# Input squares on two engines, first weights held back, rows in turn for the gates, last projection in three token parts

## The chip, the cores and the metric

The kernel runs on one core of a Trainium2 chip. The metric is the device time of one execution in microseconds (us), and a kernel's time is the median of its runs. The profile is of one execution, taken by the hardware profiler; its span starts with the first instruction and ends with the last.

Names used below: PE is TensorE (the matrix engine), PEld its weight loads, DVE is VectorE, ACT is ScalarE, POOL is GpSimd, SP is SyncE, which here only issues DMAs. SBUF is the core's memory, PSUM the eight banks into which PE writes. A DMA is issued on the queue of an engine, and an instruction that issues a DMA may first wait for a buffer to come free; everything behind it on that engine then waits too.

## The reference

The reference is a decoder trunk of two layers on 512 tokens of width 1024, all in float32. The first layer mixes tokens with a gated DeltaNet (8 query and key heads, 16 value heads of 128, chunks of 64 in the reference), the second with sliding-window attention on shared keys and values. Each layer ends with a gated channel mixer of width 2816.

```python
h = x
h = h + gated_deltanet(rmsnorm(h, a_norm_w), ...)       # layer 0
h = h + conv_gated_mlp(rmsnorm(h, ffn_norm_w[0]), ...)
k_sh, v_sh = shared_kv(h, kv_norm_w, w_kv)
h = h + sliding_window_sink_attention(rmsnorm(h, b_norm_w), k_sh, v_sh, ...)   # layer 1
h = h + conv_gated_mlp(rmsnorm(h, ffn_norm_w[1]), ...)
return rmsnorm(h, final_norm_w)

# inside gated_deltanet, after the recurrence has given o for each of the 16 value heads:
o = rmsnorm(o, out_norm_w) * silu(z)
return o.reshape(bsz, t, GDN_V_DIM) @ w_out
```

## The kernel before

Activations stand transposed, with 128 channels on the partitions and the 512 tokens along the row. A float32 product is made of three products: weights and activations are each split into a high part, rounded by ACT (`whi`, `xh`), and the rest, subtracted by DVE (`wlo`, `xl`), and PE runs high by high, high by low and low by high into one PSUM bank (`mm3`, L158 to L165). Weights come as blocks of 1024 rows by 256 columns into one of two stages (`load_stage`) and are split in halves of 128 columns (`cast`, L128 to L134) into three buffers each for `whi` and `wlo`.

An engine's order of issue comes from a scheduler that lists the instructions by priority (by default their order in the program, shifted by hand for the jobs of the first layer in `ORDER` and `SHIFT`) and takes those that its model of time holds ready. Tiles with one tag share a fixed number of buffers; a new tile of a tag takes a buffer once all uses of an older one are over.

**Input.** Four tiles of 128 tokens are loaded on SP (L204), then the first projection's weights in two halves (L210). Each tile is squared and summed along its row by ACT (L258), ACT takes the root (L259), DVE the reciprocal (L260) and the scaling (L261). PE transposes the tiles into eight rows (L266), ACT and DVE split them (L172, L173), and the projections follow.

**Gates.** The DeltaNet's outputs go to memory as `od` by chunk, the gate projections silu(z) as `zd` by head. `gate(h)` (L711 to L727) loads a head's outputs into an output row (L716) and its gate into a second row (L717), ACT scales the outputs (L720), PE transposes them (L198, `turn_row`), DVE multiplies by the gate (L723), and the result goes to memory as `yd` (L725). For the first twelve heads the output row has the tag `ol` and the gate row the tag `zl`, each with one buffer; the last four use other rows. Before the output projection of this layer, the twelve results are read back (L824) into rows `sz` (two buffers, shared with the gate projections) and `zl`, and split (L168, L169). The residual stream starts as x, loaded by columns into eight rows (L843): three of tag `f`, which has three buffers, three pieces of a third stage, and again two of tag `f`. The first six are held until the norms of heads 8 to 11 are there, by copies on POOL that read `f_c` (L839); PE transposes them (L198) and ACT copies the result (L846).

**Attention output.** The last tokens' values are split (L168, L169) while the first three tiles of the output projection are already open in the three PSUM banks of tag `d`. Their last key block of nine products (L1380) runs in three rounds over the three tiles, high by high, low by high, high by low; after a tile's last product DVE adds it to the residual (L1382). The next five tiles go through `mm3`.

**Tail.** In the last channel mixer, the last tile of the down projection (`last_down`, L962 to L964, ten blocks of three products, in two groups of six and four) is run on tokens 0 to 255 and then on 256 to 511. After each half `finish(u)` squares the new row (L1131), multiplies it by the norm's weight (L1132), adds the square to the sum over the other rows (L1133), transposes four rows for each of two token blocks (L1118, bank `d` or `s`), sums over the partitions with a column of ones (L1137), takes the root (L1138) and the reciprocal (L1139), scales the two halves of the channels on ACT (L1144) and DVE (L1146), and stores them (L1147).

Of the kernel before, what the change touches and what calls it, by code (L numbers as in the profile page):

```python
# [11 lines left out]
AF = mybir.ActivationFunctionType  # L12
ALU = mybir.AluOpType
# [4 lines left out]
P = 128  # L18
# [23 lines left out]
def kernel(  # L42
# [64 lines left out]
    def row(tag, dt=F32, n=T):  # L107
        return main.tile([P, n], dt, tag=tag, bufs=ROWS[tag], name=nm(tag))
# [4 lines left out]
    def bank(tag):  # L113
        return psum.tile([P, T], F32, tag=tag, bufs=BANKS[tag], name=nm(tag))

    def const(shape, dt=F32, s="c"):
        return cp.tile(list(shape), dt, name=nm(s))
# [87 lines left out]
        xs.append(xt)  # L205
    win = a_w_in[0]
    first = wpool.tile([P, 8, 256], F32, tag="stage", bufs=2, name=nm("stage"))
    for i in range(2):
        cs = slice(HQK * P + i * P, HQK * P + (i + 1) * P)
        SP.dma_start(first[:, :, i * P : (i + 1) * P], win[:, cs].rearrange("(k p) c -> p k c", p=P))  # L210
# [44 lines left out]
    for c in range(NC):  # L255
        junk = main.tile([P, D], F32, tag="nt", bufs=2, name=nm("junk"))
        r = const([P, 1], s="rx")
        S.activation(junk[:], xs[c], AF.Square, accum_out=r[:])  # L258
        S.activation(r[:], r[:], AF.Sqrt, bias=epsc[:, 0:1], scale=1.0 / D)  # L259
        V.reciprocal(r[:], r[:])  # L260
        V.tensor_scalar(xs[c][:], xs[c][:], r[:, 0:1], None, op0=ALU.mult)  # L261
# [447 lines left out]
    gated = {}  # L709

    def gate(h):  # L711
        ot = row("ol" if h < 12 else "dt")
        y = row("zl") if h < 12 else row(("va", "va", "us", "p6s")[h - 12])
        o3 = ot[:].rearrange("p (c e) -> p c e", c=NC)
        j = h % 4
        SP.dma_start(o3, od[h // 4, :, :, j * P : (j + 1) * P])  # L716
        SP.dma_start(y[:], zd[h])  # L717
        for c in range(NC):
            cs = slice(c * P, (c + 1) * P)
            scaled = S.activation(ot[:, cs], ot[:, cs], AF.Copy, scale=f_c[:, h, c : c + 1])  # L720
# [379 lines left out]
    def final(h, last_down):  # L1100
        hw, acc = [], None
        for k in range(KD):
            t = r2("xh")
            hw.append(t)
            if k == KD - 1:
                break
            V.tensor_scalar(t[:], h[k], onw_c[:, 9 + k : 10 + k], None, op0=ALU.mult)
            sq = r2("sum" if acc is None else "hsq")
            S.activation(sq[:], h[k], AF.Square)
            if acc is None:  # L1110
                acc = sq
            else:
                V.tensor_tensor(acc[:], acc[:], sq[:], op=ALU.add)

        def turned(hf, c, tag):
            pt = bank(tag)
            for k in range(4):
                PE.transpose(pt[:, k * P : (k + 1) * P], hw[4 * hf + k][:, c * P : (c + 1) * P], ident[:])  # L1118
            return pt

        halves = [bank("d") for _ in range(2)]
        S.activation(warm[:], acc[:, 0:1], AF.Sqrt)
        front = [turned(0, c, t) for c, t in enumerate(["s", "s", "p", "g"])]
        h7, w7 = h[KD - 1], hw[KD - 1]
        sq7 = r2("hsq")
        rt = const([P, NC], s="rt")
        ts = [slice(0, 256), slice(256, 512)]

        def finish(u):
            cs = slice(2 * u, 2 * u + 2)  # L1130
            S.activation(sq7[:, ts[u]], h7[:, ts[u]], AF.Square)  # L1131
            V.tensor_scalar(w7[:, ts[u]], h7[:, ts[u]], onw_c[:, 16:17], None, op0=ALU.mult)  # L1132
            V.tensor_tensor(acc[:, ts[u]], acc[:, ts[u]], sq7[:, ts[u]], op=ALU.add)  # L1133
            back = [turned(1, 2 * u, "d"), turned(1, 2 * u + 1, "s" if u else "d")]
            ps = bank("g")
            for c in (2 * u, 2 * u + 1):
                PE.matmul(ps[:, c : c + 1], acc[:, c * P : (c + 1) * P], onec, start=True, stop=True)  # L1137
            S.activation(rt[:, cs], ps[:, cs], AF.Sqrt, bias=epsc[:, 0:1], scale=1.0 / D)  # L1138
            V.reciprocal(rt[:, cs], rt[:, cs])  # L1139
            for c in (2 * u, 2 * u + 1):  # L1140
                for hf, pt in enumerate((front[c], back[c % 2])):
                    y = r2("xl")
                    if hf:
                        S.activation(y[:], pt[:], AF.Copy, scale=rt[:, c : c + 1])  # L1144
                    else:
                        V.tensor_scalar(y[:], pt[:], rt[:, c : c + 1], None, op0=ALU.mult)  # L1146
                    SP.dma_start(out[0, c * P : (c + 1) * P, hf * T : (hf + 1) * T], y[:])  # L1147

        def add(u):
            V.tensor_tensor(h7[:, ts[u]], h7[:, ts[u]], halves[u][:, 0:256], op=ALU.add)  # L1150
# [12 lines left out]

    def attention(h):
# [192 lines left out]
        with tc.manual_schedule(engines={mybir.EngineType.PE}):  # L1357
            stream = dense()
            for u in range(16):
                scores(u)  # L1360
                if u > 1:
                    values(u - 2)
                if u == 1:
                    take(stream, 8)
                if u > 0:
                    turn_back(u - 1)
                take(stream, 4 if u == 1 else 12 if u < 12 else 11)
            for _ in stream:
                pass
            rest = late_outputs(opened, range(begun, KD - 1))  # L1370
            take(rest, 9)
            turn_back(15)
            values(14)
            take(rest, 5)
            values(15)
            for _ in rest:
                pass
            for i in range(3):
                for m, (ps, w) in enumerate(opened):
                    PE.matmul(ps[:], w[i % 2][:, KD - 1, :], (ah, ah, al)[i][-1], start=False, stop=i == 2)  # L1380
                    if i == 2:
                        V.tensor_tensor(hT[m], hT[m], ps[:], op=ALU.add)  # L1382
        for m in range(3, KD):
            ps, w = out_tile(m)
            mm3(ps[:], w, KD, ah, al)
# [59 lines left out]
```

## Time and profile before

| | us |
|---|---|
| median of 3 runs (1415.42 to 1416.30) | 1415.86 |
| the profiled execution | 1418.66 |
| its span | 1416.8 |
| PE busy | 1384.8 |
| DVE busy | 1109.1 |
| ACT busy | 748.0 |
| POOL busy | 15.7 |

The page of the profile gives the busy time of each engine, the chain of work that ended last, the costliest groups of instructions, and the DMAs. A row of the order of time reads: start, duration, engine, line, operation, output<-input, shape, count, and in brackets how long the engine stood idle before it and what ended that. A row of the list of waits reads: engine, tile and line that waited, what it waited for, total us, times, longest. In a row of the windows come the stretch, then for each engine busy time and count, PE's granted clock, the DMAs' share and GB/s. PE's products overlap, so the pace of a row of products is read from start to start and not from the duration of one. A product of two float32 operands that are not split has two records.

### The profile page before, as it was taken

How to read it: one execution, taken by the hardware profiler on the slowest of the kernel's cores; microseconds unless marked ns; L12 is line 12 of the kernel's file. 1: busy time of each engine (PE TensorE's matmuls, PEld its weight loads, DVE VectorE, ACT ScalarE, POOL GpSimd, SP SyncE). 2: the span in 40 equal slices, each digit the busy share in tenths (PEclk: the TensorE clock that was granted, in tenths of full speed). 3: DMA queues.
4: the chain of work that ended last, by engine and by line, in shares of the span. 5: the costliest groups of instructions: out<-in, count | busy, mean ns of one | idle time of the engine just before them, and what ended most of it. 6: DMA issues, size and time to landing. Idle time of an engine off the chain costs nothing.

```text
span 1416.8 us, 21740 instructions
## 1 busy us (share of the span) xinstructions
PE 1384.8 (98%) x8362; PEld 1166.5 (82%) x8362; DVE 1109.1 (78%) x2072; ACT 748.0 (53%) x1470; POOL 15.7 (1%) x37
## 2 busy tenths in 40 slices
PE   7999999999999999999999999999999999999997
PEld 5787888878877888888988889778788888988897
DVE  4996886968856447879878889788658888878996
ACT  7764576656647325444335446567544444444543
POOL 1000000000100000000000000000000000000000
PEclk9999999999999999999999999999999999999999
DMA  5333254172465323221443223322132221432222
GB/s 160 90 104 115 80 174 124 60 230 84 143 221 157 119 86 115 90 90 46 134 149 119 75 73 108 109 76 76 60 112 86 93 90 59 137 107 86 95 75 75
DMA packets 162299, 151.80 MB, mean 107 GB/s; under 512 B 24148, under 2 KB 150677, under 8 KB 162197
## 3 DMA queue, kind: packets, MB, share of 16 engines
q1 hardware_dynamic: 159938, 150.22, 33.0%
q8 instruction: 66, 1.08, 0.3%
q10 hardware_dynamic: 2259, 0.20, 0.1%
q14 instruction: 36, 0.29, 0.1%
HBM read 133.60 MB, written 15.75 MB: 105 GB/s over the span
## 4 chain that ended last, share of the span: by engine, by line
PE 85%; DVE 7%; DMA 4%; ACT 2%; issue 1%; SPq 0%; DVEq 0%; ACTq 0%
PE d L162 20%; PE d L164 20%; PE d L163 20%; PE g L198 2%; DVE wlo L133 2%; PE d L1207 1%; PE d L1211 1%; PE d L1209 1%; PE d L1054 1%; PE d L1052 1%; PE d L1053 1%; PE s L1054 1%; PE p L1303 1%; PE s L659 1%; PE s L1052 1%
## 5 line engine op out<-in xcount | busy, mean ns | idle before, releaser
L162 PE MATMUL d<-xh,whi 128*128 128x512 f32 x1128 | 444.2, 394 | 0.2
L163 PE MATMUL d<-xl,whi 128*128 128x512 f32 x1128 | 444.0, 394 | 0.0
L164 PE MATMUL d<-xh,wlo 128*128 128x512 f32 x1128 | 442.1, 393 | 0.8 <-DVE wlo L133 0.5
L132 ACT CAST whi<-stage 128x1024 fp32r<-128x1024 f32 (+2 forms) x234 | 227.4, 976 | 249.7 <-PE d L163 170.3
L133 DVE TENSOR_TENSOR wlo<-stage,whi 128x1024 fp32r<-128x1024 f32 (+2 forms) x234 | 263.3, 1128 | 70.2 <-ACT whi L132 69.3
L164 PEld LDWEIGHTS d<-xh,wlo 128*128 128x128 f32 x1128 | 211.6, 188 | 45.5 <-DVE wlo L133 1.0
L162 PEld LDWEIGHTS d<-xh,whi 128*128 128x128 f32 x1128 | 211.7, 188 | 44.8 <-ACT xh L172 0.5
L163 PEld LDWEIGHTS d<-xl,whi 128*128 128x128 f32 x1128 | 211.7, 188 | 43.1 <-issue 0.5
L280 DVE SCALAR_TENSOR_TENSOR acc<-d,cwc,acc 128x511 f32<-128x511 f32 (+2 forms) x96 | 70.6, 738 | 8.7 <-ACT acc L277 7.8
L913 DVE TENSOR_TENSOR sz<-d,p6s 128x512 f32<-128x512 f32 x59 | 40.6, 688 | 43.4 <-PE d L164 41.2
L935 ACT ACTIVATE dt<-dt 128x512 f32<-128x512 f32 x44 | 27.8, 632 | 78.3 <-DVE dt L918 78.3
L918 DVE SCALAR_TENSOR_TENSOR dt<-sz,fcw,dt 128x511 f32<-128x511 f32 (+1 forms) x60 | 44.8, 747 | 1.8 <-ACT dt L916 0.9
L918 DVE SCALAR_TENSOR_TENSOR va<-sz,fcw,va 128x511 f32<-128x511 f32 (+1 forms) x58 | 43.3, 747 | 0.9
L561 DVE TENSOR_TENSOR sT<-sT,p6s 64x31 f32<-64x31 f32 (+15 forms) x124 | 40.9, 330 | 2.0
L555 DVE TENSOR_TENSOR p6s<-sN,sT 64x31 f32<-64x31 f32 (+15 forms) x124 | 40.7, 328 | 1.9
L1276 ACT ACTIVATE dt<-dt,sm 128x256 f32<-128x256 f32 (+1 forms) x64 | 30.1, 471 | 21.5 <-DVE sm L1259 21.5
L132 ACT CAST whi<-st 128x768 fp32r<-128x768 f32 (+1 forms) x30 | 23.7, 791 | 30.1 <-PE p L1053 5.8
L913 DVE TENSOR_TENSOR zl<-d,p6s 128x512 f32<-128x512 f32 x29 | 20.0, 688 | 17.8 <-PE d L164 17.8
L682 ACT ACTIVATE rq<-o 128x128 f32<-128x128 f32 x64 | 19.0, 301 | 25.0 <-DVE o L677 22.0
L937 DVE TENSOR_TENSOR va<-dt,va 128x512 f32<-128x512 f32 x44 | 30.4, 690 | 1.2
L133 DVE TENSOR_TENSOR wlo<-st,whi 128x768 fp32r<-128x768 f32 (+1 forms) x30 | 26.8, 899 | 2.2 <-ACT whi L132 2.2
L916 ACT ACTIVATE dt<-sz,normc,fcw 128x512 f32<-128x512 f32 x30 | 24.4, 815 | 6.5 <-DVE sz L913 6.2
(769 smaller groups left out, 2873.2 us busy)
## 6 DMA issues: line engine op xcount, KB each, us to landing
stage<-in_ffn_w_up_dram SPq DMA_DIRECT2D x44, 1024.0 KB, 4.7
stage<-in_a_w_in_dram SPq DMA_DIRECT2D x23, 1024.0 KB, 5.5
stage<-in_ffn_w_down_dram SPq DMA_DIRECT2D x16, 768.0 KB, 4.3
stage<-in_a_w_out_dram SPq DMA_DIRECT2D x8, 1024.0 KB, 5.1
st<-in_ffn_w_down_dram SPq DMA_DIRECT2D x8, 768.0 KB, 5.2
zd<-sz SPq DMA_DIRECT2D x16, 256.0 KB, 2.6
od<-o SPq DMA_DIRECT2D x16, 256.0 KB
stage<-in_b_w_q_dram SPq DMA_DIRECT2D x4, 1024.0 KB, 5.0
```

Source lines behind the costliest of these rows:

```text
L132: S.copy(hi[:, :kt, :m], src)
L133: V.tensor_tensor(lo[:, :kt, :m], src, hi[:, :kt, :m].bitcast(F32), op=ALU.subtract)
L162: PE.matmul(ps, hi[:, k, :m], xh[k], start=first and k == 0, stop=False)
L163: PE.matmul(ps, hi[:, k, :m], xl[k][:], start=False, stop=False)
L164: done.append(PE.matmul(ps, lo[:, k, :m], xh[k], start=False, stop=last and k == kt - 1))
L280: V.scalar_tensor_tensor(acc[:, d:], ps[:, : T - d], col, acc[:, d:], op0=ALU.mult, op1=ALU.add)
L555: V.tensor_tensor(tv, N[:, s, s + 1 : 32].unsqueeze(2).to_broadcast([64, n, m]), Tm[:, s : s + 1, 0:m].to_broadcast([64, n, m]), op=ALU.mult,)
L561: V.tensor_tensor(Tm[:, s + 1 : 32, 0:m], Tm[:, s + 1 : 32, 0:m], tv, op=ALU.subtract)
L913: V.tensor_tensor(u[:], ps[:], rs[:], op=ALU.mult)
L918: V.scalar_tensor_tensor(acc[:, d:], u[:, : T - d], tap(2 - d, t), acc[:, d:], op0=ALU.mult, op1=ALU.add)
L937: V.tensor_tensor(b[:], a[:], b[:], op=ALU.mult)
L1276: S.activation(ej, ej, AF.Exp, bias=ngm[:, i : i + 1], scale=-1.0, accum_out=den[:, i : i + 1])
```

## The change

Five edits:

1. The first weights are no longer issued right behind x. POOL first copies a column of the third x tile into one element of each half of the weights' stage; the loads of the halves must then wait for these copies. The identity is made before that.
2. The squares of x tiles 1 and 3 are taken by DVE with one multiply-and-sum; those of tiles 0 and 2 stay on ACT.
3. `gate(h)` takes its output row from the tags `ol` and `zl` in turn for the first twelve heads, and its gate row from tag `f`, which has three buffers.
4. The last tile of the down projection runs in three token parts of 256, 128 and 128. A part's `finish` runs behind the first group of products of the next part. The square of the new row is not added to the sum; PE sums both rows into the same bank.
5. The last key block of the three open tiles in the attention output runs tile by tile, each tile's addition right behind its three products.

```diff
     first = wpool.tile([P, 8, 256], F32, tag="stage", bufs=2, name=nm("stage"))
+    held_stage = {HQK * P: first}
+    ident = const([P, P], s="ident")
+    make_identity(nc, ident[:])
+    for i in range(2):
+        G.tensor_copy(first[:, 0, i * P : i * P + 1], xs[2][:, 0:1])
     for i in range(2):
         cs = slice(HQK * P + i * P, HQK * P + (i + 1) * P)
         SP.dma_start(first[:, :, i * P : (i + 1) * P], win[:, cs].rearrange("(k p) c -> p k c", p=P))
-    held_stage = {HQK * P: first}
-    ident = const([P, P], s="ident")
-    make_identity(nc, ident[:])
...
-        S.activation(junk[:], xs[c], AF.Square, accum_out=r[:])
+        if c % 2 == 0:
+            S.activation(junk[:], xs[c], AF.Square, accum_out=r[:])
+        else:
+            V.tensor_tensor_reduce(
+                out=junk[:], in0=xs[c][:], in1=xs[c][:], scale=1.0, scalar=0.0,
+                op0=ALU.mult, op1=ALU.add, accum_out=r[:],
+            )
...
-        ot = row("ol" if h < 12 else "dt")
-        y = row("zl") if h < 12 else row(("va", "va", "us", "p6s")[h - 12])
+        ot = row(("ol", "zl")[h % 2] if h < 12 else "dt")
+        y = row("f" if h < 12 else ("va", "va", "us", "p6s")[h - 12])
...
-        halves = [bank("d") for _ in range(2)]
+        CUTS = [(0, 2), (2, 3), (3, 4)]
+        parts = [bank("d") for _ in CUTS]
...
-        ts = [slice(0, 256), slice(256, 512)]
+        ts = [slice(a * P, b * P) for a, b in CUTS]
         def finish(u):
-            cs = slice(2 * u, 2 * u + 2)
+            c0, c1 = CUTS[u]
+            cs = slice(c0, c1)
+            V.tensor_scalar(w7[:, ts[u]], h7[:, ts[u]], onw_c[:, 16:17], None, op0=ALU.mult)
             S.activation(sq7[:, ts[u]], h7[:, ts[u]], AF.Square)
-            V.tensor_scalar(w7[:, ts[u]], h7[:, ts[u]], onw_c[:, 16:17], None, op0=ALU.mult)
-            V.tensor_tensor(acc[:, ts[u]], acc[:, ts[u]], sq7[:, ts[u]], op=ALU.add)
-            back = [turned(1, 2 * u, "d"), turned(1, 2 * u + 1, "s" if u else "d")]
+            back = [turned(1, c, "d") for c in range(c0, c1)]
             ps = bank("g")
-            for c in (2 * u, 2 * u + 1):
-                PE.matmul(ps[:, c : c + 1], acc[:, c * P : (c + 1) * P], onec, start=True, stop=True)
+            for c in range(c0, c1):
+                for x in (acc, sq7):
+                    PE.matmul(ps[:, c : c + 1], x[:, c * P : (c + 1) * P], onec, start=x is acc, stop=x is sq7)
...
-        last_down(halves[0][:, 0:256], ts[0], 0)
-        last_down(halves[0][:, 0:256], ts[0], 1)
-        add(0)
-        last_down(halves[1][:, 0:256], ts[1], 0)
-        finish(0)
-        last_down(halves[1][:, 0:256], ts[1], 1)
-        add(1)
-        finish(1)
+        n = len(CUTS)
+        for u in range(n):
+            ps = parts[u][:, 0 : ts[u].stop - ts[u].start]
+            last_down(ps, ts[u], 0)
+            if u > 0:
+                finish(u - 1)
+            last_down(ps, ts[u], 1)
+            V.tensor_tensor(h7[:, ts[u]], h7[:, ts[u]], ps, op=ALU.add)
+        finish(n - 1)
...
-            for i in range(3):
-                for m, (ps, w) in enumerate(opened):
+            for m, (ps, w) in enumerate(opened):
+                for i in range(3):
                     PE.matmul(ps[:], w[i % 2][:, KD - 1, :], (ah, ah, al)[i][-1], start=False, stop=i == 2)
-                    if i == 2:
-                        V.tensor_tensor(hT[m], hT[m], ps[:], op=ALU.add)
+                V.tensor_tensor(hT[m], hT[m], ps[:], op=ALU.add)
```

More of the change, by code (lines that the diff above doesn't have):

```diff
@@ L257 @@
         r = const([P, 1], s="rx")
-        S.activation(junk[:], xs[c], AF.Square, accum_out=r[:])
+        if c % 2 == 0:
+            S.activation(junk[:], xs[c], AF.Square, accum_out=r[:])
+        else:
+            V.tensor_tensor_reduce(
+                out=junk[:],
+                in0=xs[c][:],
+                in1=xs[c][:],
+                scale=1.0,
+                scalar=0.0,
+                op0=ALU.mult,
+                op1=ALU.add,
+                accum_out=r[:],
+            )
         S.activation(r[:], r[:], AF.Sqrt, bias=epsc[:, 0:1], scale=1.0 / D)
@@ L1126, in final @@
         rt = const([P, NC], s="rt")
-        ts = [slice(0, 256), slice(256, 512)]
+        ts = [slice(a * P, b * P) for a, b in CUTS]
         def finish(u):
-            cs = slice(2 * u, 2 * u + 2)
+            c0, c1 = CUTS[u]
+            cs = slice(c0, c1)
+            V.tensor_scalar(w7[:, ts[u]], h7[:, ts[u]], onw_c[:, 16:17], None, op0=ALU.mult)
             S.activation(sq7[:, ts[u]], h7[:, ts[u]], AF.Square)
-            V.tensor_scalar(w7[:, ts[u]], h7[:, ts[u]], onw_c[:, 16:17], None, op0=ALU.mult)
-            V.tensor_tensor(acc[:, ts[u]], acc[:, ts[u]], sq7[:, ts[u]], op=ALU.add)
-            back = [turned(1, 2 * u, "d"), turned(1, 2 * u + 1, "s" if u else "d")]
+            back = [turned(1, c, "d") for c in range(c0, c1)]
             ps = bank("g")
-            for c in (2 * u, 2 * u + 1):
-                PE.matmul(ps[:, c : c + 1], acc[:, c * P : (c + 1) * P], onec, start=True, stop=True)
+            for c in range(c0, c1):
+                for x in (acc, sq7):
+                    PE.matmul(ps[:, c : c + 1], x[:, c * P : (c + 1) * P], onec, start=x is acc, stop=x is sq7)
             S.activation(rt[:, cs], ps[:, cs], AF.Sqrt, bias=epsc[:, 0:1], scale=1.0 / D)
             V.reciprocal(rt[:, cs], rt[:, cs])
-            for c in (2 * u, 2 * u + 1):
-                for hf, pt in enumerate((front[c], back[c % 2])):
+            for c in range(c0, c1):
+                for hf, pt in enumerate((front[c], back[c - c0])):
                     y = r2("xl")
```

2 lines of the change are left out of this document (removed).

## The prediction

> **What bounds the kernel now.** I read the page's engine shares first, then its chain of waits, then the list of what TensorE (PE) waited for, and only then the order of time at the four places that the diff touches.
>
> ```profile
> PE 1384.8 (98%) x8362; PEld 1166.5 (82%) x8362; DVE 1109.1 (78%) x2072; ACT 748.0 (53%) x1470; POOL 15.7 (1%) x37
> PE 85%; DVE 7%; DMA 4%; ACT 2%; issue 1%; SPq 0%; DVEq 0%; ACTq 0%
> ...
> PE g L235 <- DMA xt<-in_x_dram: 8.5, 1, 8.5
> ...
> PE d L162 <- ACT kT L168: 2.0, 1, 2.0
> ...
> PE g L198 <- ACT ol L720: 1.5, 1, 1.5
> PE p L659 <- ACT us L653: 1.5, 1, 1.5
> ```
>
> PE is busy 98% of a span of 1416.8 us and holds 85% of the chain that ended last. So a saving on another engine counts only where PE waits: 32 us in all, and the list shows the singles (columns: total, times, longest). The change goes at four of them: the input (8.5 us before PE's first work), the gates (1.5, L198), the last key block of the attention output (short waits, its rows stand below), and the tail, which is no wait in this list but the time after the last projection's final product. It leaves the number of products as it is, except in the tail, where one half of the tokens is cut in two. All sums are made in the profiled execution (its time 1418.66, 2.8 above the median of 1415.86; its span 1416.8) and carried over to that median as differences.
>
> **Input: squares on two engines, weights held.** The order of time at the start:
>
> ```profile
> 4.27 1.06 ACT L258 ACTIVATE junk<-xt 128x1024 f32<-128x1024 f32 x1 [1.39 <-DMA xt<-in_x_dram]
> 5.70 1.06 ACT L258 ACTIVATE junk<-xt 128x1024 f32<-128x1024 f32 x1 [0.28 <-DMA xt<-in_x_dram]
> 8.16 1.06 ACT L258 ACTIVATE junk<-xt 128x1024 f32<-128x1024 f32 x1 [0.94 <-DMA xt<-in_x_dram]
> 9.73 1.05 ACT L258 ACTIVATE junk<-xt 128x1024 f32<-128x1024 f32 x1
> 11.11 1.03 ACT L132 CAST whi<-stage 128x1024 fp32r<-128x1024 f32 x1
> 11.44 0.75 DVE L261 TENSOR_SCALAR xt<-xt,rx 128x1024 f32<-128x1024 f32 x1
> 12.17 1.23 DVE L133 TENSOR_TENSOR wlo<-stage,whi 128x1024 fp32r<-128x1024 f32 x1
> ...
> SPq L210 <- DMA xt<-in_x_dram: 2.0, 2, 1.0
> ...
> 1003.43 0.48 DVE L1259 CUSTOM_DVE_ANT_0 dt<-s,sz,nsink 128x256 f32<-128x256 f32 x1 [1.45 <-PE s L1251]
> ```
>
> ScalarE (ACT) squares the four tiles one after the other; the third begins at its landing (8.16), the fourth right behind the third's root. The fourth tile is scaled at 11.44 to 12.19, and PE's first projection follows. With the weights held until the third tile is there, the third lands earlier: the first two landed 1.43 apart (4.27, 5.70), so a third at the same distance is at about 7.1, one microsecond sooner. That is the best case, -1.0. Against it: squares two and four move to VectorE (DVE). No row shows this operation at 1024 columns; a two-operand pass over 1024 (L133) has 1.23, and the same operation over 256 (L1259) has 0.48, four times that 1.9; L133 is the nearer, so I take 1.3. DVE then owes, from 5.70 on, two squares (2.6), four scalings with their reciprocals (4 x 0.9, 0.75 of it the scaling) and one short copy: 6.2 us and the copy, so the fourth tile is scaled at about 12.2, as now. If the order of issue puts the third tile's scaling ahead of the fourth square, one gap of about 0.8 is added. Bounds -1.0 and +0.8; I take **0**, because the serial work on DVE alone leads to the present time.
>
> The two holding copies on GpSimd (POOL) wait for the third tile; what can stand behind them there are memsets for later stages. The two weight transfers (512 KB each) are issued at about 7.5 instead of at the landings of the first two tiles. SyncE (SP) already waits there for x (2.0 us, L210). [...] Behind them on SP stand small constants (conv weights, gate biases) that nothing in this stretch waits for.
>
> **Gates: two rows for outputs, three for gates.** Before, one output row and one gate row served twelve gates:
>
> ```profile
> 299.52 1.28 ACT L720 ACTIVATE ol<-ol,fc 128x128 f32<-128x128 f32 x4 [3.02 <-DMA ol<-od]
> 299.98 1.21 PE L198 MATMUL g<-ident,ol 128*128 128x128 f32 x4 [1.52 <-ACT ol L720]
> ...
> SPq L717 <- DMA yd<-zl: 8.5, 4, 3.7
> ...
> L839 POOL COPY f<-fc x3: 180/180/253, 359.7 to 360.0; 128x1 f32<-128x1 f32 x3
> ...
> L198 PE MATMUL g<-ident,f x20: 271/273/327, 448.4 to 454.9; 128*128 128x128 f32 x20
> ...
> 419.27 6.26 DMA sz<-yd
> ```
>
> A gate's load of the gate row waits until the store of the gate before has landed (8.5 us of SP's queue between 200 and 300 us, with weight loads stuck behind it), and its output load waits for the transposes before. With rows in turn both loads start a gate earlier. ACT's 3.02 goes, and with it PE's one wait of **1.52**. The other waits of ACT and DVE on these rows end beside a PE that has other products; removing them yields nothing. The rows come from tag f, which the first three x rows of the residual (loaded at 360 until now) need next. They must then wait for the stores of the last three of these gates, which are out before yd is read back at 419. PE wants the rows only from 448.4 (L198 on f), so 29 us cover the delay, unless it hits that reload (below). I take **-1.5**; bounds -5.0 (also PE's 2.0 and 1.5 for L168 and L653, both short of 430, go, since SP is no longer blocked there) and +2.8 (-1.5 and the 4.3 of the first rival).
>
> **Attention output: each tile closed at once.** The three tiles' last nine products ran in the order hi, lo, hi by tile; now each tile runs its three.
>
> ```profile
> 1014.75 0.69 DVE L169 TENSOR_TENSOR at<-p,at 128x512 fp32r<-128x512 f32 x1 [6.44 <-ACT at L168]
> 1015.06 0.85 PE L1380 MATMUL d<-at,whi 128*128 128x512 f32 x3
> ...
> 1016.44 0.84 PE L1380 MATMUL d<-at,whi 128*128 128x512 f32 x3
> ...
> 1016.87 2.95 ACT L132 CAST whi<-stage 128x1024 fp32r<-128x1024 f32 x3 [2.14 <-PE d L1380]
> ...
> 1016.87 1.88 DVE L1382 TENSOR_TENSOR h<-h,d 128x512 f32<-128x512 f32 x3 [1.42 <-PE d L1380]
> 1018.67 3.49 DVE L133 TENSOR_TENSOR wlo<-stage,whi 128x1024 fp32r<-128x1024 f32 x3
> ...
> 1020.44 0.39 PE L164 MATMUL d<-sy,wlo 128*128 128x512 f32 x1
> ```
>
> The first tile's third product now begins at 1016.44; it will begin two products (0.46) after 1015.06, at 1015.52, and its operand is ready at 1015.44, so no new wait. What this releases comes 0.92 earlier: the weight buffer for the next cast (ACT 1016.87) and the first addition (DVE 1016.87). The second and third additions wait for their own products, to about 1018.0 in place of 1018.7, so DVE's weight passes start 0.65 earlier. PE has only six products to do between 1017.1 and 1020.44 and gains between those: **-0.9**, bounds -0.4 and -1.6 (weights ahead of the last addition).
>
> **Tail: three parts of 256, 128, 128 tokens.**
>
> ```profile
> 1402.92 0.28 PE L962 MATMUL d<-ktok,whi 128*128 128x256 f32 x1
> ...
> 1405.08 1.03 PE L1118 MATMUL d<-ident,xh 128*128 128x128 f32 x8
> 1405.95 0.50 PE L1137 MATMUL g<-ones,ol 128*128 128x1 f32 x4
> 1406.32 0.36 PE L962 MATMUL d<-sy,whi 128*128 128x256 f32 x1
> ...
> 1407.83 0.49 PE L1118 MATMUL d<-ident,xh 128*128 128x128 f32 x3
> ...
> 1408.32 0.41 DVE L1150 TENSOR_TENSOR pz<-pz,d 128x256 f32<-128x256 f32 x1
> ...
> 1409.78 0.58 PE L1137 MATMUL g<-ones,ol 128*128 128x1 f32 x4 [0.17 <-DVE ol L1133]
> ...
> 1410.39 0.26 ACT L1138 ACTIVATE rt<-g,eps 128x2 f32<-128x2 f32 x1 [1.22 <-PE g L1137]
> ...
> 1411.56 0.74 DVE L1146 TENSOR_SCALAR xl<-g,rt 128x512 f32<-128x512 f32 x1
> ...
> 1413.01 0.40 SPq L1147 DMA_DIRECT2D out_dram<-xl  x1
> ...
> 922.10 0.18 PEld L1251 LDWEIGHTS s<-kT,rq 64*128 64x128 f32 x1 [0.35 <-issue]
> ...
> 922.21 0.19 PEld L1251 LDWEIGHTS s<-kT,rq 64*128 64x128 f32 x1
> ```
>
> A part of the projection is 30 products, 18 and 12. At 256 columns one takes 0.12 (18 from 1402.92 to 1405.08). At 128 columns no full product of this kind is in the trace. Two rows bound it: products of one column with 128 weight columns still take 0.37 / 4 = 0.093 (L1137), and in the scores products of 128 columns follow the weight loads of one half of the array at 0.11 (922.10, 922.21). So the weight load holds the pace, not the columns; I take 0.11, bounds 0.06 (half of 0.12, columns alone) and 0.12. [...]
>
> PE from 1402.92 to its last product, before 4.91 (2.16 + 0.87 + 0.37 + 1.51). After: 60 products x 0.11 = 6.6, twelve transposes 1.31, twelve summing records 1.11 (two operands in place of one; two records to a product): 9.0. That is +4.1. Behind the last product: before, to the last result written, 1407.83 to 1412.30 = 4.47. After, on one column block: 0.49 to the addition, 0.3 for it, 0.3 for the square with the scaling beside it, 0.1 of gaps, 0.6 for two summing records, 0.5 for root and reciprocal, 0.75 for one result in place of two: 3.0, so -1.45. SP issues its last stores 0.5 apart and the last of four goes out 0.7 behind the last result (1413.01 after 1412.30); with two it is about 0.45: -0.25. The three parts hold all three d banks, so the transposes of the second column block wait for a bank until a result of the first is out; PE has the products of the later parts meanwhile, so I cost that at 0. Without that cover PE would stand for a root, a reciprocal and a result, 1.3 us. The tail is **+2.4**; bounds -0.6 (0.06 a product) and +3.0 (0.12).
>
> **Sum:** 0 - 1.5 - 0.9 + 2.4 = 0.0, hence 1415.9 us.
>
> **Rivals.** *Slower, the x rows.* Where their loads are issued on SP between the last gate stores and the load of yd at 419.27, six rows of 256 KB at the pace of the x tiles (three times 1.43) put 4.3 us in front of it; it already takes 6.26 and PE already waits 2.0 for the split behind it. Then +4.3: 1420.2. That load has no slack, so it costs from the first row issued ahead of it, 0.7 us a row. For it: POOL's holding copies are in order, so the three rows of the other tag wait behind the last f row. Against it: PE needs the rows 29 us later, so any later place on SP costs nothing. *Short products stream at their columns' pace.* At 0.06 the tail is -0.6, the sum 1412.9. Against it: the two rows above. [...] *Faster, the stalls before the output projection go.* Then -3.5 more: 1412.4. For it: SP is blocked by the single gate row there as well. Against it: the wait for L168 follows a load into a row (sz) shared with the last gate's projection, which the change leaves. *The holding does nothing.* SP already holds these transfers for x (2.0 us); if the third tile lands no sooner than 8.16, DVE's square of the fourth ends late: +0.8, 1416.7.
>
> **How the numbers follow.** Forecast 0.55 (own range 1413.4 to 1418.4); x rows 0.16; short products free 0.08; stalls gone 0.10; holding idle 0.11. The range takes the low ends of the two faster rivals and most of the slow one: 1412.2 to 1420.2. A measurement here tells about 0.2% (2.8 us) from no change: faster than 1413.0 has the stalls, half of the free products: 0.14; slower than 1418.7 the x rows and the tail's upper bound beside a gate gain that fails: 0.19; the rest, 0.67, is the same.
>
> **What would show it.** The products at 128 columns in the last projection: start to start 0.11 (right) or 0.06. PE's wait on L198 at 300 gone. The first addition behind the attention output 0.9 earlier against the product before it. The fourth tile's scaling at 12.2 or so. A new wait of PE for the split of yd near 425 would be the first rival; a PE that waits in the tail for a bank would break the tail's sum.

## The result, and the profile after

| | before | after |
|---|---|---|
| median of 4 runs, us | 1416.08 | 1433.30 |
| lowest to highest | 1415.42 to 1416.94 | 1431.05 to 1434.56 |
| the profiled execution | 1418.66 | 1434.56 |
| its span | 1416.8 | 1432.7 |

The change makes the kernel slower: 1.0113 times the time before, 95% interval 1.0100 to 1.0127, some 17 us. The forecast was 1415.9 in a range that ended at 1420.2, so the time lies far outside. Lines of the kernel after stand 15 to 17 higher than before.

To find where the time went, the start of the same instruction is read in both orders of time (us from the span's start):

| instruction | before | after | later by |
|---|---|---|---|
| first product of the first projection | 13.6 | 15.6 | 2.0 |
| first product of the keys | 47.2 | 52.9 | 5.7 |
| first chunk's output `o` | 157.4 | 163.5 | 6.1 |
| last `o` of the recurrence | 435.6 | 435.5 | -0.1 |
| first addition behind the output projection | 455.9 | 470.1 | 14.2 |
| last one | 525.2 | 541.4 | 16.2 |
| last block of the attention output | 1015.1 | 1030.2 | 15.1 |
| last down projection | 1391.0 | 1404.9 | 13.9 |
| last result | 1411.6 | 1428.1 | 16.5 |
| span | 1416.8 | 1432.7 | 15.9 |

So the loss has two places: 6 us before 164 us, and 8 to 10 us around 435 to 541 us. The attention output gained 1.2 and the tail lost 2.0 to the end of the span, as forecast in kind. The engines' shares and PE's list of waits after (it stands beside the one in the prediction; columns: total, times, longest):

```profile
PE 1394.4 (97%) x8400; PEld 1172.3 (82%) x8400; DVE 1113.7 (78%) x2077; ACT 747.5 (52%) x1469; POOL 16.5 (1%) x39
```

```profile
PE d L162 <- ACT kT L168: 8.0, 1, 8.0
PE g L238 <- DMA xt<-in_x_dram: 7.9, 1, 7.9
PE d L164 <- DVE wlo L133: 3.3, 2, 2.8
...
PE g L198 <- ACT ol L736: 0.2, 1, 0.2
```

The wait on L198 is gone but for 0.2, as forecast. The wait for the split of `yd` (L168) has grown from 2.0 to 8.0, and a wait of 2.8 on the low weights is new. PE also shows 9.6 us more of busy time (1394.4 against 1384.8), too much for the 38 records added; a product at half clock counts as longer work (near 48 us one of 512 columns has 0.63 in place of 0.39).

**The start.** After, in order of time:

```profile
7.08 0.75 POOL L215 COPY stage<-xt 128x1 f32<-128x1 f32 x2 [5.35 <-DMA xt<-in_x_dram]
7.77 3.20 DVE L277 TENSOR_SCALAR xt<-xt,rx 128x1024 f32<-128x1024 f32 x1
8.63 1.80 POOL L410 MEMSET Xg<- 128x2048 f32 x1
9.39 1.28 ACT L335 ACT_TABLE_LOAD   x1 [0.68 <-issue]
10.90 1.28 ACT L275 ACT_TABLE_LOAD   x1
10.97 1.20 DVE L265 CUSTOM_DVE_ANT_0 junk<-xt 128x1024 f32<-128x1024 f32 x1
13.44 0.75 DVE L277 TENSOR_SCALAR xt<-xt,rx 128x1024 f32<-128x1024 f32 x1
14.85 0.68 ACT L172 ACTIVATE xh<-s,normc 128x512 fp32r<-128x512 f32 x1
...
15.58 0.79 PE L162 MATMUL d<-xh,whi 128*128 128x512 f32 x1 [0.21 <-ACT xh L172]
```

The third x tile landed near 7.0 and a square on DVE takes 1.20: both as the prediction took them (7.1 and 1.3). But the memsets that now stand behind the holding copies run beside a scaling on DVE, which takes 3.20 in place of 0.75, and the exponential of `nega` slips between two roots, so that ACT loads its tables twice (1.28 each). The fourth tile's scaling begins at 13.44 and ends at 14.19; the prediction had it done at 12.2. The first split of x begins 1.41 behind the start of that scaling (14.85), before 1.45 behind it (12.89 after 11.44).

**At 45 us.** The next rows are a product of the kernel before and one of the kernel after, in order of time, then windows of the kernel after (PE's granted clock is the number behind POOL's):

```profile
45.96 0.48 PE L235 MATMUL g<-ident,f 128*128 128x128 f32 x2 [1.72 <-DVE onwc L237]
```

```profile
45.75 0.50 PE L164 MATMUL d<-xh,wlo 128*128 128x512 f32 x1 [2.75 <-DVE wlo L133]
```

```profile
44.00:46.00 2.00, 0.25 (x1) 0.25 (x2) 1.97 (x5) 1.95 (x4) 0.00 (x0) 1.00 0.00 0
46.00:48.00 2.00, 2.00 (x8) 1.59 (x8) 1.94 (x3) 1.06 (x2) 0.00 (x0) 0.75 0.04 9
48.00:50.00 2.00, 2.00 (x7) 1.52 (x6) 1.46 (x2) 0.00 (x0) 0.00 (x0) 0.50 0.85 248
50.00:52.00 2.00, 2.00 (x13) 1.51 (x12) 0.93 (x4) 1.08 (x2) 0.00 (x0) 0.90 1.07 378
```

After, PE stands for 2.75 us, and then its clock is at half: the last three windows lose 0.5, 1.0 and 0.2 us, 1.7 together. Before, PE stood here too, for 1.72 us, and its clock stayed at 1.00. So the wait itself is only 1.0 longer.

**At 435 us.** First SP's queue before, then SP's queue, ACT and PE after, in order of time, and the windows after:

```profile
414.83 0.41 SPq L824 DMA_DIRECT2D sz<-yd  x1
416.50 0.32 SPq L706 DMA_DIRECT2D zd<-sz  x1
```

```profile
434.02 0.63 ACT L721 ACTIVATE sz<-d 128x512 f32<-128x512 f32 x1
...
436.59 0.38 SPq L722 DMA_DIRECT2D zd<-sz  x1
437.02 0.49 SPq L840 DMA_DIRECT2D sz<-yd  x1
...
442.65 0.62 ACT L168 CAST kT<-sz 128x512 fp32r<-128x512 f32 x1 [3.66 <-DMA sz<-yd]
443.32 0.80 PE L162 MATMUL d<-kT,whi 128*128 128x512 f32 x1 [7.95 <-ACT kT L168]
```

```profile
435.00:440.00 5.00, 0.37 (x4) 0.18 (x2) 1.36 (x5) 2.78 (x10) 0.00 (x0) 0.61 0.97 288
440.00:445.00 5.00, 1.67 (x3) 0.73 (x3) 0.69 (x1) 1.22 (x4) 0.00 (x0) 0.50 0.75 249
445.00:450.00 5.00, 5.00 (x20) 3.84 (x20) 2.25 (x3) 4.41 (x16) 0.00 (x0) 0.52 0.75 248
```

Before, the last gate projection was done by 416 and the first read-back into `sz` was issued at 414.83; products of the output projection then filled PE's gaps in the last steps of the recurrence. After, the last gate projection itself is that filler: its silu ends at 434.65, its store goes out at 436.59, and the read-back, behind it on SP, at 437.02. When the recurrence ends at 435 PE has nothing left. It waits 6.0 us longer than before, and the half clock behind that costs about 3.3 (0.85 from 443.3 to 445, 2.4 to 450). Less the 1.3 of L198 that is 8.0, and the table has 8.1 (14.2 less 6.1). The three x rows in tag `f` were issued between 400.2 and 408.4 and delay nothing.

**Attention output and tail.** After, in order of time:

```profile
1030.18 0.39 PE L1397 MATMUL d<-at,whi 128*128 128x512 f32 x1
...
1031.16 1.38 DVE L1398 TENSOR_TENSOR h<-h,d 128x512 f32<-128x512 f32 x2 [0.59 <-PE d L1397]
...
1416.87 0.22 PE L978 MATMUL d<-ktok,whi 128*128 128x128 f32 x1
...
1428.06 0.75 DVE L1165 TENSOR_SCALAR xl<-g,rt 128x512 f32<-128x512 f32 x1
```

The first addition comes 0.98 behind the first product (1.81 before). From the first short block (1416.87; 1402.92 before) to PE's last product there are 9.35 us (4.91 before); a product of 128 columns takes 0.11.

### The profile page after: what moved, and what is told of

Its sections match the earlier page's. It is cut to its first block, busy times and chain, and to the rows that moved or that the text cites. A ratio compares the mean times of both kernels' runs of the same rounds, so it can differ in the third digit from the quotient of the medians.

```text
span 1432.7 us, 21815 instructions
## 1 busy us (share of the span) xinstructions
PE 1394.4 (97%) x8400; PEld 1172.3 (82%) x8400; DVE 1113.7 (78%) x2077; ACT 747.5 (52%) x1469; POOL 16.5 (1%) x39
## 4 chain that ended last, share of the span: by engine, by line
PE 83%; DVE 7%; DMA 4%; ACT 3%; issue 1%; SPq 0%; POOL 0%; ACTq 0%; DVEq 0%
PE d L162 18%; PE d L163 18%; PE d L164 18%; DVE wlo L133 2%; PE g L198 1%; PE d L1070 1%; PE d L1224 1%; PE d L1068 1%; PE d L1228 1%; PE d L1226 1%; PE d L1069 1%; PE s L1070 1%; PE s L1068 1%; PE s L1069 1%; DMA stage<-in_a_w_in_dram 1%
```

## The experiments

The theory formed on this: nothing in the five edits costs much by its own work; the scheduler lists the instructions in another order, at two places. The rivals: an edit's own work costs it (the table load, the x rows), or a sum of small costs does. A kernel that has one part of the change is named p_ and the part. Ratios are to the kernel before in the same rounds, whose median was 1417.4 to 1418.6 us.

### One part alone

`p_input` has edits 1 and 2, `p_gate` edit 3, `p_tail` edit 4, `p_attn` edit 5.

> The kernel before with edits 1 and 2 alone (weights held, squares of x tiles 1 and 3 on DVE). Theory A (the start is late and the rest follows from it): PE's first projection product about 2 us later than before, as in the changed kernel, and the two stalls behind it (PE waiting 2.8 us for a weight pass of DVE near 45 us, 8 us in front of the output projection) come with it: 1428 to 1434 us. Rival B (the stalls belong to the gates' rows): only the late start is seen, 1417 to 1419 us, and PE's granted clock stays at 1.0 from 60 us on.

> The kernel before with edit 3 alone (rows in turn for the gates). Theory A: PE's wait for the split in front of the output projection stays near 2 us and the 1.5 us for L198 at 300 us goes: 1413 to 1416 us. Rival B (the gates' rows bring the last gate projection and the reload behind it about 20 us late): the wait of 8 us is here, with a granted clock of about 0.5 behind it: 1424 to 1430 us.

> The kernel before with edit 4 alone (three token parts). By the prediction's sum +2.4 us: 1418.3 us. If the time behind the last product falls by what was counted and the products of 128 columns follow at about 0.06 us, -0.6: 1415.3 us. The changed kernel's own profile has to tell the pace as well.

> The kernel before with edit 5 alone (each of the three open tiles closed at once). By the prediction's sum -0.9 us: 1415.0 us. Rival: PE's wait behind these products has another last cause, and the time stays within 0.3 us of 1415.9.

| | median, us | ratio | 95% interval |
|---|---|---|---|
| p_input | 1428.32 | 1.0074 | 1.0056 to 1.0092 |
| p_gate | 1427.86 | 1.0071 | 1.0056 to 1.0086 |
| p_tail | 1421.65 | 1.0025 | 1.0014 to 1.0035 |
| p_attn | 1418.43 | 0.9994 | 0.9982 to 1.0006 |

The parts don't add up: 10.9, 10.4 and 4.2 us above the before of the same rounds make 25.5, the whole change 17. The gates alone bring the wait of 7.9 us for L168 and an output projection that is 8.3 late. But the input alone also changes what is issued around 415 us, 400 us behind the edit: its first addition is 16.0 late. Six of that are won back, and its attention output is 10.0 late. By the first product of the keys it is 5.9 late, and between 418 and 425 us half clock costs 3.4 us, with no wait of PE over 0.84. The kernel after has full clock there, so it does not pay this share. And 1.7 us of clock near 46 us are lost in the profiles of `p_input`, `p_gate` and `p_tail` alike, and once in the kernel after; in `p_gate` and `p_tail` that is ahead of anything the edit touches.

In the tail alone the clock falls to half while PE is busy without a gap (windows of p_tail, then products):

```profile
1406.80:1407.80 1.00, 1.00 (x10) 0.98 (x10) 1.00 (x3) 0.93 (x2) 0.00 (x0) 1.00 0.00 0
1407.80:1408.80 1.00, 1.00 (x11) 1.00 (x10) 0.55 (x3) 0.31 (x1) 0.00 (x0) 0.91 0.78 301
1408.80:1409.80 1.00, 1.00 (x6) 1.00 (x5) 0.00 (x0) 0.00 (x0) 0.00 (x0) 0.50 1.04 404
...
1413.80:1414.80 1.00, 1.00 (x7) 1.00 (x7) 0.50 (x2) 0.22 (x1) 0.00 (x0) 0.50 1.07 412
```

```profile
1408.37 0.28 PE L963 MATMUL d<-kT,whi 128*128 128x128 f32 x1
1408.48 0.28 PE L964 MATMUL d<-kT,wlo 128*128 128x128 f32 x1
...
1408.99 0.41 PE L964 MATMUL d<-sy,wlo 128*128 128x128 f32 x1
1409.20 0.41 PE L962 MATMUL d<-sy,whi 128*128 128x128 f32 x1
```

The products go from 0.11 apart to 0.21, which costs about 3.5 us up to PE's last product. The kernel after ran the same products at full clock.

### The gates: one order

`g_fill` is edit 3 and one dependency: the third step of the last recurrence pass is issued behind the last product of the last gate projection. `g_f` is edit 3 with the old output row; only the gate row goes to tag `f`.

```diff
 # g_fill
+    behind(st[3]["first", 2], passes[QKV + 256 * 7 + P][-1])
 # g_f
-        ot = row(("ol", "zl")[h % 2] if h < 12 else "dt")
+        ot = row("ol" if h < 12 else "dt")
```

> Edit 3 alone, and the third step of the last recurrence pass is issued on PE behind the last gate projection's final product. Theory A (with the new rows the scheduler lets the recurrence run ahead and spends the last gate projection as filler between its steps, so that the output projection has no operands when the recurrence ends): the reload of yd comes near 415 us again, PE's wait of 7.9 us in front of the output projection shrinks to 2 us or less, the granted clock stays at 1.0 there, and the time is 1413 to 1418 us. Rival B (the rows themselves hold the reload up): the wait moves but stays, 1424 to 1430 us.

> Half of edit 3: the gate row takes tag f, the output row keeps the single buffer of tag ol. Theory A2 (it takes both halves to let the gates, and with them the recurrence, run ahead): no long wait in front of the output projection, 1413 to 1418 us. Rival: the rows of tag f alone, which the x rows need next, hold the reload up: 1424 us and more.

`g_fill`: 1417.95 us, 0.9993 (0.9984 to 1.0001). SP issues the read-back ahead of the last gate's store again, and the wait is 1.2 (order of time of g_fill on SP, then its list of PE's waits):

```profile
417.99 0.38 SPq L826 DMA_DIRECT2D sz<-yd  x1
421.06 0.32 SPq L707 DMA_DIRECT2D zd<-sz  x1
```

```profile
PE d L162 <- ACT kT L168: 1.2, 1, 1.2
```

One ordering edge takes some 11 us away (1.0071 to 0.9993), with every row and load of edit 3 still there: this loss is the order's, shown. `g_f` missed: 1423.68, 1.0031 (1.0019 to 1.0043). The read-back goes out at 410.81, earlier than before, and no wait in this stretch is over 0.7 us, yet PE runs some 10 us at half clock (windows of g_f):

```profile
410.00:415.00 5.00, 3.49 (x74) 2.76 (x64) 2.35 (x5) 3.14 (x5) 0.30 (x1) 0.76 0.54 161
415.00:420.00 5.00, 4.29 (x18) 4.00 (x19) 3.40 (x5) 2.34 (x4) 0.00 (x0) 0.50 0.77 229
420.00:425.00 5.00, 5.00 (x21) 4.26 (x20) 3.00 (x7) 1.79 (x10) 0.00 (x0) 0.72 0.92 306
```

The lost share of the clock is 1.2, 2.5 and 1.4 us: 5.1, the whole of its loss. What lets the clock fall there stays open.

### The input: what it costs, and what its order costs

`in_exp` is edits 1 and 2 with the exponential of `nega` behind the last root; `p_sq` is edit 2 alone; `p_hold` edit 1 alone.

> Edits 1 and 2 alone, and the exponential of the decay's constant (L335) is issued on ACT behind the last root. Theory A (the two table loads in front of the last root make the start late, and that lateness starts the rest): no table load between the roots, PE's first projection product at 13.6 to 14.3 us in place of 16.2, and the time comes back to 1415 to 1420 us. Rival B (what costs is the new order of issue behind the start, not the start itself): the first product is early, and the time stays at 1425 to 1430 us.

> Edit 2 alone (squares of x tiles 1 and 3 on DVE, weights issued right behind x as before). If DVE's share of the squares costs about nothing, as predicted: fourth tile scaled at 11.4 to 12.4 us and 1414 to 1418 us. If the holding of the weights is the part that does no harm and the squares are, 1424 us and more.

> Edit 1 alone. Theory (the third tile lands a microsecond sooner, the weights some two later, and the scheduler, which takes the weights for late, splits them behind the splits of x): first projection product at 14.5 to 16 us, 1418 to 1422 us. Rival (the holding gains its microsecond): first product before 13.6 us, 1414 to 1417 us.

`in_exp`: 1428.48, 1.0069 (1.0057 to 1.0082). The table loads are gone from between the roots, the first product is still at 15.8, now behind a scaling of 3.21, and the wait of 2.7 stays: the table loads are not what the 10 us hang on. `p_sq`: 1428.86, 1.0067 (1.0051 to 1.0083). It has no holding copies, and its fourth tile is scaled from 11.84 to 12.59 (forecast: done at 12.2). But on ACT two casts of weights now stand ahead of the first split of x, one of them waiting for its load (p_sq, then `sq_ord` of below, in order of time):

```profile
13.74 0.51 ACT L132 CAST whi<-gst 128x384 fp32r<-128x384 f32 x1 [1.50 <-DMA gst<-in_a_w_in_dram]
14.16 1.04 ACT L132 CAST whi<-stage 128x1024 fp32r<-128x1024 f32 x1
15.11 0.68 ACT L172 ACTIVATE xh<-s,normc 128x512 fp32r<-128x512 f32 x1
```

```profile
13.12 0.69 ACT L174 ACTIVATE xh<-s,normc 128x512 fp32r<-128x512 f32 x1 [0.92 <-PE s L281]
...
16.39 0.50 ACT L134 CAST whi<-gst 128x384 fp32r<-128x384 f32 x1
```

`p_hold`: 1422.57, 1.0033 (1.0022 to 1.0045), with its first product only at 19.9 (forecast 14.5 to 16): the first weights are cast at 18.77, behind six splits of x. It has no squares on DVE, but the long scaling:

```profile
8.22 3.25 DVE L264 TENSOR_SCALAR xt<-xt,rx 128x1024 f32<-128x1024 f32 x1
9.12 1.80 POOL L397 MEMSET Xg<- 128x2048 f32 x1
```

So the long scaling is edit 1's and the order of the casts edit 2's. In `p_input` no scaling took over 1.06 us; there two table loads ahead of the last root put the fourth scaling at 13.95 and the first product at 16.2. Each of the three makes the start about 2 us late, and where one is gone another holds it. To test the order alone, `sq_ord` is edit 2 with three ACT instructions put behind the splits of x where they stood before, and `in_ord` the same on edits 1 and 2:

```diff
+    behind(made[-1], halves_hi[4])        # the gates' weights behind the 5th split of x
-    S.activation(nega[32:48, :], gp16[32:48, 0:1], AF.Exp)
+    behind(S.activation(nega[32:48, :], gp16[32:48, 0:1], AF.Exp), halves_hi[6])
+    behind(made[2], halves_hi[7])         # the second projection's weights behind the 8th
```

> Edit 2 alone, with three instructions of ACT put back to their place in the order of issue of before: the split of the gates' weights behind the fifth split of x, the exponential of the decay's constant behind the seventh, the second projection's weights behind the eighth. Theory A (DVE's squares cost nothing themselves; the scheduler, which takes the x tiles for later than they are, moves weight splits and a table change ahead of the splits of x, and everything behind shifts): first projection product at 13.6 to 14.3 us, no wait of 2.7 us near 45, 1415 to 1419 us. Rival (the squares on DVE cost through DVE's time): 1424 us and more.

> Edits 1 and 2 with the same three instructions put back. If holding the weights costs nothing more: 1415 to 1419 us and a first product at 13.6 to 14.3 us. Rival: the memsets that stand behind the two holding copies on POOL run beside DVE's scaling, which takes 3.2 us in place of 0.75 as in the changed kernel's profile: first product about 1.5 to 2.5 us later than without the holding, 1418 to 1422 us.

`sq_ord`: 1418.58, 1.0003 (0.9990 to 1.0016). Its first product (13.9) and first key product (47.4) are both 0.2 later than before, and its first addition stands at 455.9 again. Three ACT instructions of the first 20 us set the order at 415 us too, and are worth some 9 us (1.0067 to 1.0003). In the profiled execution of `p_sq`, the slowest of its four, 6.2 us are lost by the first key product (53.4) and 5.1 by half clock between 418 and 430 us; `sq_ord` has neither. `in_ord`: 1420.01, 1.0013 (1.0001 to 1.0024): with the order kept, holding brings nothing; it stands 1.4 us above `sq_ord` in the same rounds, though the intervals overlap.

`in_mem` and `all_mem` (edits 1 and 2, and all five with both orders) put POOL's memset of `Xg` and its select ahead of the holding copies, and the cast of the first weights ahead of the splits.

> Edits 1 and 2 with ACT's three instructions put back and POOL's memsets ahead of the holding copies. Theory A: first projection product at 13.2 to 14.0 us and 1415.5 to 1418.5 us, 1 to 2 us under the run with the memsets behind (1420.0). Rival: the holding costs by the later weights, first split of the weights after 12 us and 1419 us and more.

> All five edits with both orders put back, and the memsets that stood behind the two holding copies on POOL issued ahead of them (the first weights' split stays ahead of the splits of x). Theory A (DVE's scaling stands while POOL works through its memsets): no scaling above 0.8 us, first projection product at 13.4 to 14.2 us in place of 15.6, 1418 to 1421 us, some 2 us under the run without it (1422.8). Rival (something else makes this scaling long, say the x tile's landing): it stays at 3.2 us, and the time within 1 us of 1422.8.

`in_mem`: 1421.30, 1.0023 (1.0013 to 1.0034). `all_mem`: 1421.79, 1.0020 (1.0009 to 1.0030). Both lie above their forecasts; what came true for `in_mem` is its rival, the later weights. In order of time in `all_mem`:

```profile
7.79 0.95 DVE L279 TENSOR_SCALAR xt<-xt,rx 128x1024 f32<-128x1024 f32 x1
...
13.80 1.04 ACT L134 CAST whi<-stage 128x1024 fp32r<-128x1024 f32 x1 [3.45 <-DMA stage<-in_a_w_in_dram]
```

The scaling of 3.2 is gone, but the weights are now issued at 9.42, 4.4 us ahead of their cast, and ACT waits 3.45 us for them; the first product is at 15.5. The holding copy is early beside the memsets or late behind them, and neither beats no holding.

### All five with the orders, and the best of it

`all_ord` is the whole change with both orders, `best2` that without edit 4, `tail2` edit 4 with two parts of 256, `best5` edits 1, 2 and 5 with order, memsets ahead and `tail2`, `best1` edits 3 and 5 with the order of `g_fill`.

```diff
-        CUTS = [(0, 2), (2, 3), (3, 4)]
+        CUTS = [(0, 2), (2, 4)]
```

> All five edits, with the three instructions of ACT put back and the third step of the last recurrence pass behind the last gate projection's final product. Theory A (of the 17 us some 14 are order of issue): 1417 to 1423 us, the rest above before being the tail's 2 us (more where the clock falls in it) and up to 2 us of the start. Rival (the edits cost together what the order of each hides): 1426 us and more.

> As the run with all five edits and both orders put back, without edit 4 (the last projection in two halves as before). Theory A: 2 to 4 us less than with the three parts, 1414 to 1419 us. Rival: the parts cost nothing beside the rest, within 1 us of the run with them.

> Edit 4 with two parts of 256 tokens in place of three: its finish and its order stay, the products of 128 columns go. Theory A (the price is the 128 columns: twelve more products of the weights' pace each, and a clock that falls while they run): 1415.0 to 1418.0 us, no more than the kernel before, and a granted clock of 1.0 to PE's last product. Rival (the new finish costs, by its second summing product and its place behind the next part's first group): 1419 us and more.

> Edits 1, 2 and 5 with the order of ACT put back and POOL's memsets ahead of the holding copies, and edit 4 with two parts of 256 tokens; the gates as before. Theory A: the small gains of the parts add up, the holding 0.5, the attention output 1, the finish 0.5: 1413 to 1417 us. Rival: each is too small to be seen beside the changes of clock from run to run: within 0.1% of before.

> Edits 3 and 5 with the third step of the last recurrence pass behind the last gate projection's final product; input and tail as before. Theory: -0.9 of the attention output and 0 to -1.5 of the gates, 1414 to 1417 us where before has 1416 to 1418, a ratio of 0.998 to 0.9995. Rival: nothing that can be measured, a ratio whose interval holds 1.

| | median, us | ratio | 95% interval |
|---|---|---|---|
| all_ord | 1422.81 | 1.0034 | 1.0022 to 1.0046 |
| best2 | 1419.35 | 1.0012 | 0.9998 to 1.0027 |
| tail2 | 1419.37 | 1.0005 | 0.9993 to 1.0017 |
| best5 | 1421.11 | 1.0019 | 1.0008 to 1.0031 |
| best1 | 1416.78 | 0.9987 | 0.9976 to 0.9999 |

Four ordering edges bring the whole change from 1.0113 to 1.0034. They also part the two losses of the start. `all_ord` and `best2` still have the long scaling and a first product at 15.6, as the kernel after. But their wait near 45 us is the one of before (1.85 and 1.86, on the copy), and the first product of the keys stands at 49.5, not at 52.9. So the 2.0 us of the start are the memsets', and what follows on them is the order's. The rest of `all_ord` is the tail (`best2` without it: 1.0012) and, argued and not shown, the holding. `tail2` and `best5` lie above their forecasts. `best1` is 1.4 us faster than before (1418.22 in its rounds); its interval ends just under 1, it is the best of several, and 0.13% is below the 0.2% named in the prediction, so the gain is likely and not sure.

## Why the prediction was wrong, step by step

- **Input, 0 with bounds of -1.0 and +0.8: the step that failed.** The landing and the square came as worked out, and in `p_sq` the fourth scaling ends 0.4 behind the forecast. Two sentences did not hold. "The serial work on DVE alone leads to the present time" took ACT's order as given; the casts and the exponential moved ahead of the splits of x. And "what can stand behind them there are memsets for later stages" priced those at nothing, though they run beside DVE's scaling (3.20 for 0.75). In the kernel after the memsets make PE's start 2.0 us late. The order of the casts brings the wait of 2.75 at 45 us in place of 1.72, 1.7 of clock behind it, and the other order at 415 us (`p_sq` against `sq_ord`: some 9 us in all). The weights took 4.4 us from their issue to their cast in `all_mem` (9.42 to 13.80), and the 0 has no term for that.
- **Gates, -1.5 with bounds of -5.0 and +2.8: the second.** L198's wait went as forecast. "Removing them yields nothing" counted the other waits as covered and left the order of everything else as it was. With gates that are served sooner the recurrence is issued ahead and the last gate projection becomes its filler; the read-back shares its row and queue with that, and is 22 us later. That the wait for L168 hangs on a row shared with the last gate's projection stood in the prediction, as an argument that it would stay; it was the place to ask what the wait becomes if that projection moves.
- **The rival of the x rows** named the right victim and the wrong cause: the rows were issued by 408.4 and cost nothing, the store of the last gate stood ahead. At +4.3 it was under half of the loss at this place, 6.0 of wait and 3.3 of clock, and it had no clock in it.
- **Attention, -0.9.** The first addition is 0.83 nearer to the first product (forecast 0.92), and 1.2 is gained to the last down projection. In time alone `p_attn` can't be told from no change.
- **Tail, +2.4.** PE +4.44 (forecast +4.1), behind its last product -1.88 (forecast -1.45), stores -0.6 (forecast -0.25): +2.0. The pace of 0.11 held, the rival at 0.06 fell. `p_tail` lies 4.2 above the before of its rounds (interval 2.0 to 5.0), some 2 more than the sum; its half clock, which the sum took as full, cost 3.5 in the profiled execution, enough for that. Whether every execution has it is not shown. Three parts against two cost about 2.8 us (1.0025 against 1.0005, on different chips, with intervals that overlap a little).
- **The sum** added the parts. They share one order and are not independent.

Open: why the scheduler's model of time prefers these orders was not taken apart, nor what lets the clock fall without a long wait, nor the 2.0 us between the first and last addition, which `p_gate` shows too.

## What to carry over

Where a list scheduler with a model of time sets the order, an edit is not worth its own durations: compare the order of issue of the two builds on every engine, far behind the edit too, before a price is put on it, and pin the few instructions that must stay. In this kernel one edge or three were worth some 9 to 11 us, and the edits themselves 1 to 3. Read PE's granted clock wherever the order has changed: each fall to half lost about 1.7 us or a multiple of it in these runs, and some came without a long wait.

## What was not expected of the hardware

**The clock falls with and without a gap.** It fell to 0.50 behind waits of 2.75 and 7.95 us (above). In `p_tail` it fell with PE busy in every microsecond, and in `g_f` with no wait over 0.7 us: a long gap of PE explains neither. The length of a wait alone does not decide. PE's wait near 45 us for DVE's copy left the clock at 1.00 in ten profiles (1.59 to 1.80 us) and half clock followed in five (1.81 to 1.88), but near 427 us a wait of 2.68 in `p_attn` kept the clock and one of 2.67 in `tail2` lost it. The size is regular: read in windows of 1 us, each stretch of half clock ahead of 1400 us costs 1.7 us (near 46 in nine profiles, at other places in four), 3.4 (`p_input`, `in_exp`), 5.1 (`p_sq`, `g_f`) or 6.8 (after and `p_gate`, from 430 us, partly in PE's wait). In the kernel after, the stretches run from 47.0 to 50.4 and from 436.1 to 449.8 us, 3.4 us and four times that. No run here shows what starts one or sets its length.

**A scaling on DVE lasts through a row of POOL's memsets.** The scaling of 1024 columns takes 0.75 alone and 3.20 to 3.28 in the five kernels where POOL's row of memsets begins beside it (after, `in_exp`, `p_hold`, `all_ord`, `best2`), ending 0.5 behind the `Xg` memset each time (10.97 against 10.43 after). It does not end between two of them: after, the second memset of the row is over at 8.64, and the scaling, begun at 7.77, at 10.97. A scaling that began inside the `Xg` memset took 1.06 (`p_input`) and 0.98 (`in_ord`) and also ended 0.5 behind it. What holds DVE there was not shown.
